# Moving the sample units of the third attention group into the mix stage, in a hybrid decoder step on eight cores

## The chip, the cores and the metric

The program runs on all eight cores of one Trainium2 chip; each core takes half a prompt sequence and four of the 32 sample sequences. The metric is the device time of the slowest core in microseconds (us). In the profiles PE is TensorE (matrix products; PEld its weight loads), DVE is VectorE, ACT ScalarE, POOL GpSimd and SP SyncE; here the last two mostly issue loads. TensorE writes its results to PSUM banks, from which DVE or ScalarE *evicts* them. Cores 0 to 3 are one die, 4 to 7 the other. Most executions agree within a fraction of a per cent, but the program also has a slow state, in which the cores of a die show a lower granted clock and the time is some per cent longer. Spans and stage lengths come from the profile of one execution, which covers every core.

## The reference, cut to what matters

One decoder layer. A wide input projection gives a GLU branch (depthwise convolution, layer norm, `w_pw`), queries, keys and values of three head groups with dilations 1, 4 and 16, and two gates. The branches are mixed, projected by `w_out`, and followed by a SwiGLU FFN.

```python
z = h @ w_in                               # [glu | q | k | v | gate_conv | gate_attn]
conv_out, new_conv = conv_branch(u, u_past, w_dw, b_dw, ln_g, ln_b, w_pw, b_pw)
o_att, new_k, new_v = attend(q, k, v)      # three groups, combined per head
attn_out = o_att @ w_o_att
x = x + (gate_conv * conv_out + gate_attn * attn_out) @ w_out
x = x + (silu(hf @ w_gate) * (hf @ w_up)) @ w_down
```

The four new tokens of each sample sequence attend to cached keys and values. The kernel cuts this into *units*: for each group 17 K units (load a 128x512 piece of the key cache and a broadcast query row, multiply, reduce), one exponential, and 17 V units (load a piece of the value cache, weight it, add it up by a small matmul). A K unit loads 512 KB, a V unit 256 KB. Group 1 shares some pieces; groups 2 and 3 load every one, so group 3 loads about 13 MB.

## The kernel before

The stages in order of time are: q and K/V passes of groups 1, 2 and 3; the GLU stage with the convolution; layer norm; the mix stage (48 iterations of gates, `w_pw` product, `w_o` product); `w_out`; FFN. Each engine has one instruction list and executes it in order (for DVE the timeline below shows it), so a wait in front of an instruction holds up everything behind it. All unit loads go through one issuing queue (SP), and units are put into *slots* between the other instructions:

```python
seq = [('K',) + u for u in cunits(0)]
for g in (0, 1):                             # V units of one group alternate with K units of the next
    seq.append(('E', g, 0, 0))
    for u0, u1 in zip(cunits(g), cunits(g + 1)):
        seq += [('V',) + u0, ('K',) + u1]
seq += [('E', 2, 0, 0)] + [('V',) + u for u in cunits(2)]
# ... K and Q have three buffers each, V two
def unit_slot(budget=1.4):                   # about one K unit with one V unit, or two V units
    u_pe()                                   # small matmuls of finished V units
    while used < budget and ...:
        u_prefetch()                         # loads, up to six units ahead, as far as buffers are free
        u_do(tptr['do'])                     # DVE work of this unit
    u_prefetch()
```

So K units of group 3 ran in its K/V pass and its V units in the GLU stage:

```python
# K/V passes of groups 2 and 3
def qslot():   ...  if qs[0] in (3, 5, 7): unit_slot()
def kslotA(i): if g == 1 or i > 0:  unit_slot()
def kslotB(i): if g == 1 or i >= 8: unit_slot()
# GLU stage: in each of 8 channel blocks x 3 column groups
unit_slot()
if tptr['do'] == len(seq) and n < 7:  ...    # then the sample normalisation
if n == 0 and ti > 0:
    prompt_norm(2 * ti - 2); prompt_norm(2 * ti - 1)   # load a denominator row, multiply
```

The mix stage used two alternating pairs of PSUM banks and loaded `w_pw` and `w_o` together per block of 256 columns. The `w_out` stage read chunks of 512 columns, two at a time; the first two were loaded during mix.

```python
b0, b1 = 4 + 2 * q, 5 + 2 * q                # mix(it), q = it % 2
if it == 35: wo.append(load_out(0))
if it == 41: wo.append(load_out(1))
# after mix: load_out(2), load_out(3), then 8 MB of residual rows
for p in range(2):
    for t in range(8):
        for c in (2 * p, 2 * p + 1):
            acc_rows(t, c, ...)
```

The softmax here doesn't subtract the row's maximum and nothing guards it: scores larger than these inputs give would overflow.

## Time and profile before

| | before |
|---|---|
| time, median of the first three runs | 2130.14 us (2126.32 to 2364.76; the longest is a slow run) |
| spans of the eight cores in the profile | 2097.5 to 2133.8 us |
| TensorE busy, slowest core | 2006.9 us, 94% |

Three lines of the page of the slowest core (core 3): busy time and share of TensorE, then the busy tenths of TensorE and the granted clock in 40 slices of 53 us (counted from 0 below).

```profile
PE 2006.9 (94%) x12908; PEld 1176.8 (55%) x12908; DVE 792.7 (37%) x1378; ACT 411.2 (19%) x764; POOL 132.8 (6%) x140
...
PE   5899989996779999999999999999999999999996
...
PEclk9999999998889999999999999999999999999998
```

TensorE is the bottleneck, and after the start it loses time mainly in slices 9 to 11, about 480 to 640 us: the third group's K/V pass and the GLU stage. The windows view of these two stages on core 3 (window, its length, busy time and instructions of TensorE, weight loads, DVE, ScalarE and GpSimd; then clock, DMA share, GB/s):

```profile
361.40:524.70 163.30, 146.88 (x835) 92.24 (x833) 76.87 (x181) 42.41 (x86) 4.56 (x4) 0.95 0.72 141
524.70:719.50 194.80, 161.06 (x1299) 93.55 (x1298) 69.37 (x112) 39.91 (x78) 9.13 (x8) 0.91 0.57 109
```

The chain of waits there (start, length, what) is mostly loads for units:

```profile
450.65 11.44 DMA t_67<-ck
...
476.00 12.71 DMA t_66<-ck
...
491.68 12.20 DMA t_73<-cv
...
506.10 15.74 DMA t_68<-sqkv
...
546.67 5.72 DMA t_130<-dnd
...
557.78 11.01 DMA t_131<-dnd
```

`ck` and `cv` are the caches, `sqkv` the new sample rows, `dnd` the softmax denominators of the prompt. The timelines of DVE and TensorE on core 3 show how such a wait arrives there, and that it is paid twice (in brackets the idle time before an instruction, and what ended it):

```profile
488.87 0.69 DVE L212 TENSOR_TENSOR t_74<-t_66,t_69 128x512 f32<-128x512 f32 x1 [4.25 <-DMA t_66<-ck]
...
490.75 0.26 DVE L212 TENSOR_TENSOR t_58<-ps,t_58 128x64 f32<-128x64 f32 x1
```

```profile
484.68 3.67 PE L212 MATMUL ps<-t_54,t_56 128*128 128x512 bf16 x16
491.15 0.63 PE L212 MATMUL ps<-t_90,t_95 128*128 128x64 bf16 x4 [2.81 <-DVE t_58 L212]
...
492.68 5.96 PE L212 MATMUL ps<-t_55,t_56 128*128 128x512 bf16 x16
```

DVE waits 4.25 us for a key load before it can do the work that TensorE needs (`t_58`). TensorE idles 2.81 us behind DVE, and the next sixteen matmuls of this size span 5.96 us instead of 3.67. The windows view shows why, a granted clock (third figure from the end) of 0.50:

```profile
490.60:497.40 6.80, 6.25 (x21) 2.78 (x22) 3.30 (x9) 1.38 (x3) 0.00 (x0) 0.50 0.92 114
```

The Trainium skill, page "TensorE: Matmul & The Clock Gate", section "Why this matters for your kernels", advises against idle gaps above about 3 us because the clock then drops; here 2.8 us (up to the modelled end of the matmul before) were followed by that lower clock.

### The profile page before, as it was taken

The page shows a single profiled execution, that of the slowest core. Times are in us where ns is not written, and L with a number is a line of the kernel's source. Part 1 is how long each engine was busy: PE and PEld are TensorE (multiplying, and loading weights), DVE is VectorE, ACT ScalarE, POOL GpSimd, SP SyncE. Part 2 cuts the span into 40 slices and gives each one's busy share as a digit, 9 for nine tenths or more (in the row PEclk, how much of TensorE's full clock was granted, in tenths as well). Part 3 has the DMA queues.
Part 4 walks back from the last instruction along what each step waited for, and adds up shares of the span by engine and source line. Part 5 has one row for each costly group of instructions (what it writes and reads, how often), then busy time and mean ns, then how long its engine had stood idle before and what let it go on. Part 6 is the DMA issues. An engine that isn't in the chain of part 4 may idle for free.

```text
span 2133.8 us, 34104 instructions; the slowest of 8 cores (2097.5 to 2133.8 us)
## 1 busy us (share of the span) xinstructions
PE 2006.9 (94%) x12908; PEld 1176.8 (55%) x12908; DVE 792.7 (37%) x1378; ACT 411.2 (19%) x764; POOL 132.8 (6%) x140
## 2 busy tenths in 40 slices
PE   5899989996779999999999999999999999999996
PEld 3454544663445556666545655656556556565652
DVE  4544564454324372222225143241441432414125
ACT  4353221321112252222104200000000000000012
POOL 0100000000000101101000000000000000000000
PEclk9999999998889999999999999999999999999998
DMA  8849788668548774747593999879879786454403
GB/s 217 159 123 152 113 159 139 117 156 157 133 78 137 110 99 56 107 56 102 107 229 45 184 157 184 133 138 172 139 139 164 127 152 97 71 78 63 79 23 138
DMA packets 228534, 266.31 MB, mean 125 GB/s; under 512 B 8867, under 2 KB 192803, under 8 KB 223229
## 3 DMA queue, kind: packets, MB, share of 16 engines
q0 software_dynamic: 190080, 130.03, 45.6%
q1 hardware_dynamic: 33686, 86.02, 15.6%
q10 hardware_dynamic: 4608, 48.08, 9.6%
q8 instruction: 106, 1.74, 0.3%
q14 instruction: 54, 0.44, 0.1%
HBM read 369.64 MB, written 60.30 MB: 201 GB/s over the span
## 4 chain that ended last, share of the span: by engine, by line
PE 83%; DMA 7%; DVE 4%; issue 3%; ACT 2%; SPq 1%; ACTq 1%; DVEq 0%; POOL 0%; POOLq 0%
PE ps L212 83%; DMA t_53<-w_in 1%; DMA t_73<-cv 1%; DMA t_68<-ck 1%; DMA t_68<-sqkv 1%; SPq L233 1%; DMA t_66<-ck 1%; DMA t_67<-ck 1%; DMA t_131<-dnd 1%; DMA t_59<-xext 1%; ACTq L233 0%; DMA t_125<-t_127 0%; DVE t_138 L212 0%; DVE t_63 L212 0%; DVE t_137 L212 0%
## 5 line engine op out<-in xcount | busy, mean ns | idle before, releaser
L212 PE MATMUL ps<-t_56,t_53 128*128 128x347 bf16 (+3 forms) x1152 | 180.4, 316 | 10.1 <-DVE t_127 L212 9.2
L212 PE MATMUL ps<-t_56,t_54 128*128 128x347 bf16 (+3 forms) x1152 | 183.3, 319 | 3.7 <-ACT t_157 L212 1.1
L212 PEld LDWEIGHTS ps<-t_56,t_53 128*128 128x128 bf16 x1152 | 112.9, 99 | 73.3 <-issue 13.9
L212 PEld LDWEIGHTS ps<-t_56,t_54 128*128 128x128 bf16 x1152 | 114.0, 100 | 68.7 <-issue 7.4
L212 PE MATMUL ps<-t_55,t_56 128*128 128x512 bf16 (+1 forms) x640 | 150.7, 390 | 0.0
L212 PE MATMUL ps<-t_54,t_56 128*128 128x512 bf16 (+1 forms) x640 | 145.4, 381 | 1.1 <-DVE t_56 L212 1.1
L212 ACT ACTIVATE t_192<-ps 128x347 f32<-128x347 f32 (+1 forms) x66 | 30.3, 460 | 535.9 <-PE ps L212 535.9
L212 PE MATMUL ps<-t_53,t_56 128*128 128x512 bf16 (+1 forms) x432 | 105.6, 400 | 4.6 <-DMA t_53<-w_in 4.6
L212 PEld LDWEIGHTS ps<-t_55,t_56 128*128 128x128 bf16 (+1 forms) x640 | 75.3, 122 | 57.7 <-issue 11.4
L212 PEld LDWEIGHTS ps<-t_54,t_56 128*128 128x128 bf16 (+1 forms) x640 | 74.9, 122 | 53.6 <-issue 4.0
L212 PE MATMUL ps<-t_136,wh_175 128*128 128x347 bf16 (+1 forms) x576 | 91.0, 311 | 0.5 <-DVE t_136 L212 0.5
L212 PE MATMUL ps<-t_136,wh_174 128*128 128x347 bf16 (+1 forms) x576 | 90.9, 311 | 0.0
L212 PE MATMUL ps<-t_136,wh_176 128*128 128x347 bf16 (+1 forms) x576 | 90.8, 311 | 0.0
L212 PE MATMUL ps<-t_136,wh_173 128*128 128x347 bf16 (+1 forms) x576 | 90.8, 311 | 0.0
L212 ACT ACTIVATE t_193<-ps 128x347 f32<-128x347 f32 (+1 forms) x66 | 30.3, 459 | 277.8 <-PE ps L212 277.8
L212 PE MATMUL ps<-t_136,wh_169 128*128 128x347 bf16 (+1 forms) x480 | 75.7, 311 | 0.0
L212 PE MATMUL ps<-t_136,wh_171 128*128 128x347 bf16 (+1 forms) x480 | 75.7, 311 | 0.0
L212 PE MATMUL ps<-t_136,wh_170 128*128 128x347 bf16 (+1 forms) x480 | 75.7, 311 | 0.0
L212 PE MATMUL ps<-t_136,wh_172 128*128 128x347 bf16 (+1 forms) x480 | 75.7, 311 | 0.0
L212 PEld LDWEIGHTS ps<-t_53,t_56 128*128 128x128 bf16 (+1 forms) x432 | 42.7, 102 | 57.7 <-issue 17.6
L212 DVE TENSOR_TENSOR t_190<-ps,t_192 128x347 bf16<-128x347 f32 (+1 forms) x36 | 18.7, 520 | 149.1 <-PE ps L212 149.1
L212 DVE TENSOR_TENSOR t_190<-ps,t_193 128x347 bf16<-128x347 f32 (+1 forms) x36 | 18.7, 520 | 147.7 <-PE ps L212 147.7
(408 smaller groups left out, 2910.8 us busy)
## 6 DMA issues: line engine op xcount, KB each, us to landing
t_54<-w_in POOLq DMA_DIRECT2D x14, 1024.0 KB, 15.4
t_53<-w_in POOLq DMA_DIRECT2D x12, 1024.0 KB, 13.9
kso<-ck ACTq DMA_DIRECT2D x8, 1016.0 KB, 11.4
vso<-cv ACTq DMA_DIRECT2D x8, 1016.0 KB, 10.0
t_59<-xext SPq DMA_DIRECT2D x6, 1024.0 KB, 10.0
t_53<-w_in POOLq DMA_DIRECT2D x12, 512.0 KB, 16.1
t_60<-xext SPq DMA_DIRECT2D x6, 1024.0 KB, 8.3
wh_175<-w_gate POOLq DMA_DIRECT2D x6, 1024.0 KB, 10.1
```

The source lines that it names most:

```text
L212: self.q[eng].append(lambda e: getattr(e, meth)(*a, **kw).then_inc(s, 1))
L233: self.q[queue].append(lambda e: e.dma_start(out=out, in_=in_, **kw).then_inc(s, 16))
```

## The change

The intent is to take the third group's units out of the stretch that stalls and put them into the mix stage, where DVE is mostly idle (busy 4.4 of 19.2 us in the windows view). Their buffers are columns of `hT` (now called `yA`) that nobody needs any more; V units of this group get three buffers instead of two. To make room, `w_o` is loaded whole and early, in the GLU stage; the mix stage uses one pair of PSUM banks; the sample rows' `w_o` product follows at the end of mix. As the whole `w_o` lies where the first `w_out` chunk used to go, only one chunk is loaded during mix, and the first pass of `w_out` takes chunk 0 for all rows and then chunk 1. Denominator rows are asked for earlier, and the unit slots move.

```diff
+seq = [('K',) + u for u in cunits(0)] + [('E', 0, 0, 0)]
+for u0, u1 in zip(cunits(0), cunits(1)):
+    seq += [('V',) + u0, ('K',) + u1]
+seq += [('E', 1, 0, 0)] + [('V',) + u for u in cunits(1)]
+n_early = len(seq)
+seq += [('K',) + u for u in cunits(2)] + [('E', 2, 0, 0)] + [('V',) + u for u in cunits(2)]
...
-    last = q_pass(g, pre, qslot)
+    last = q_pass(g, pre, nothing)
-    if g == 1 or i >= 8:                     # second slot of a block
+    if g == 1 or i >= 5:
...
-    unit_slot()                              # in the GLU stage
-    if n == 0 and ti > 0:
-        prompt_norm(2 * ti - 2); prompt_norm(2 * ti - 1)
+    if n == 1: prompt_norm(ti)               # loads issued in the first block, four buffers
+    if n == 2 and ti == 0: prompt_norm(3)
...
+    if ph == 2: S.dma('pool', wo4, w_o...)   # whole w_o
...
-    b0, b1 = 4 + 2 * q, 5 + 2 * q            # mix; now PS[4] and PS[5] only
+    if it > ND: unit_slot(1.4, len(seq))     # ND = 9
...
-    if it == 35: wo.append(load_out(0))
-    if it == 41: wo.append(load_out(1))
+    if it == 41: wo.append(load_out(0))
+wo.append(load_out(1))                       # after the last iteration
+mix_sample()                                 # 64 products with 16 columns
...
-    for t in range(8): for c in (2 * p, 2 * p + 1): ...
+    # p == 0: c = 0 for all t, then c = 1 for all t; p == 1 as before
```

More of the change, by code (lines that the diff above doesn't have):

```diff
@@ L527, in cunits, with ubuf @@
             return [(g, s, i) for s in range(4) for i in range(4)] + [(g, 4, 0)]
-        seq = [('K',) + u for u in cunits(0)]
-        for g in (0, 1):
-            seq.append(('E', g, 0, 0))
-            for u0, u1 in zip(cunits(g), cunits(g + 1)):
-                seq += [('V',) + u0, ('K',) + u1]
-        seq += [('E', 2, 0, 0)] + [('V',) + u for u in cunits(2)]
+        seq = [('K',) + u for u in cunits(0)] + [('E', 0, 0, 0)]
[4 more added lines that the diff above has]
+        seq += [('K',) + u for u in cunits(2)] + [('E', 2, 0, 0)] + [('V',) + u for u in cunits(2)]
         bufs, free, users = [], [], {}
-        ctr = {'K': -1, 'Q': -1, 'V': -1}
+        ctr = {}
         for t, (kind, g, s, i) in enumerate(seq):
             fresh = not (g == 0 and s < 4 and i > 0)
+            late = g == 2
             b_ = {}
-            fr = -1
-            for nm, n_, new in (('K', 3, fresh), ('Q', 3, True)) if kind == 'K' else (('V', 2, fresh),) if kind == 'V' else ():
+            fr = n_early - 1 if late else -1
+            for nm, n_, new in (('K', 3, fresh), ('Q', 3, True)) if kind == 'K' else (('V', 3 if late else 2, fresh),) if kind == 'V' else ():
+                c_ = ctr.get((nm, late), -1) + (1 if new else 0)
+                ctr[(nm, late)] = c_
                 if new:
-                    ctr[nm] += 1
-                    fr = max(fr, users.get((nm, ctr[nm] % n_), -1))
-                b_[nm] = ctr[nm] % n_
-                users[(nm, b_[nm])] = t
+                    fr = max(fr, users.get((nm, late, c_ % n_), -1))
+                b_[nm] = c_ % n_
+                users[(nm, late, c_ % n_)] = t
             bufs.append(b_)
             free.append(fr)
+        yA = v3(S.sbuf('yA', H_, 16 * HP), 16)
+        def ubuf(nm, g, i):
+            if g < 2:
+                return {'K': uK, 'Q': uQ, 'V': uV, 'P': [uP], 'PV': uPV}[nm][i]
+            if nm == 'PV':
+                return hT[:, 10 + i // 2, 512 * (i % 2):512 * (i % 2) + 512]
+            return yA[:, {'K': 0, 'Q': 3, 'V': 6, 'P': 9}[nm] + i, 0:512]
         def u_load(t):
@@ L553, in u_load @@
             if kind == 'K':
-                Q_, K_ = uQ[b_['Q']], uK[b_['K']]
+                Q_, K_ = ubuf('Q', g, b_['Q']), ubuf('K', g, b_['K'])
                 if s == 4:
@@ L562, in u_load @@
             elif kind == 'V':
-                V_ = uV[b_['V']]
+                V_ = ubuf('V', g, b_['V'])
                 if s == 4:
@@ L573, in u_do @@
             if kind == 'K':
-                P_ = uP[0:np_]
-                S.op('dve', lambda e: e.tensor_tensor(out=P_, in0=uK[b_['K']][0:np_], in1=uQ[b_['Q']][0:np_], op=ALU.mult))
+                P_ = ubuf('P', g, 0)[0:np_]
+                S.op('dve', lambda e: e.tensor_tensor(out=P_, in0=ubuf('K', g, b_['K'])[0:np_], in1=ubuf('Q', g, b_['Q'])[0:np_], op=ALU.mult))
                 dst = SnA[0:64, g, :] if s == 4 else ScA[:, g, 16 * s + 4 * i:16 * s + 4 * i + 4]
@@ L589, in u_do @@
                 pc = PnA[0:64, g, :] if s == 4 else PcA[:, g, 16 * s + 4 * i:16 * s + 4 * i + 4]
-                PV_ = uPV[pv_][0:np_]
-                S.op('dve', lambda e: e.tensor_tensor(out=v3(PV_, 4), in0=v3(uV[b_['V']][0:np_], 4), in1=mkap(pc, [[1, 4], [0, 128]]), op=ALU.mult))
+                PV_ = ubuf('PV', g, pv_)[0:np_]
+                S.op('dve', lambda e: e.tensor_tensor(out=v3(PV_, 4), in0=v3(ubuf('V', g, b_['V'])[0:np_], 4), in1=mkap(pc, [[1, 4], [0, 128]]), op=ALU.mult))
                 upend.append((uslot[0], PV_, g, s, i))
@@ L598, in build_program @@
         avail = [False] * 3
+        late_ok = [False]
         def u_pe(lag=2):
@@ L608, in u_prefetch, with unit_slot @@
         def u_prefetch():
-            while tptr['load'] < len(seq) and tptr['load'] <= tptr['do'] + 6 and avail[seq[tptr['load']][1]] and free[tptr['load']] < tptr['do']:
+            while tptr['load'] < len(seq) and tptr['load'] <= tptr['do'] + 6 and avail[seq[tptr['load']][1]] and free[tptr['load']] < tptr['do'] and (tptr['load'] < n_early or late_ok[0]):
                 u_load(tptr['load'])
                 tptr['load'] += 1
-        def unit_slot(budget=1.4):
+        def unit_slot(budget=1.4, lim=None):
             uslot[0] += 1
@@ L617, in unit_slot @@
             used = 0.0
-            while used < budget and tptr['do'] < len(seq) and avail[seq[tptr['do']][1]]:
+            while used < budget and tptr['do'] < (lim or n_early) and avail[seq[tptr['do']][1]]:
                 u_prefetch()
@@ L825, in pre @@
                     fin[0]()
-            qs = [0]
-            def qslot():
-                qs[0] += 1
-                if qs[0] in (3, 5, 7):
-                    unit_slot()
             def kslotA(i):
@@ L850, in build_program @@
         dgc = [ab(w2t + 1568 + 512 * i, 512).rearrange("p (q c) -> p q c", c=32) for i in range(2)]
-        PcS = v3(af(w2t + 2592, 512), 16)
         wtap = v3(af(w2t + 3104, 256), 8)
@@ L854, in build_program @@
         ysum, ysq = v3(af(R, 1056), 2), v3(af(R + 1056, 1056), 2)
-        stT = [v3(af(R + 10240, 480), 4), v3(af(w2t + 3376, 480), 4)]
-        cps = af(R + 11264, 1024)
-        osn = ab(R + 12288, 256)
+        stT = [v3(af(R + 5120 + 480 * i, 480), 4) for i in range(2)]
+        cps = af(R + 7334, 1024)
+        wo4 = v3(ab(R + 8448, 4096), 4)
         uc = [v3(af(R + 20552 + 136 * i, 136), 4) for i in range(2)]
@@ L862, in build_program @@
         sg = af(R + 20192, 360)
-        rdb = [af(R + 16688 + 1024 * i, 1024) for i in range(2)]
-        PnS, rds = af(R + 21752, 4), af(R + 21756, 4)
-        yA = v3(S.sbuf('yA', H_, 16 * HP), 16)
+        rdb = v3(af(R + 8448, 4096), 4)
+        PcS = v3(yA[:, 12, 0:512], 16)
+        osn = hT[:, 13, 0:512]
+        ta_s, cv_s = v3(yA[:, 14, 0:256], 16), v3(yA[:, 14, 256:512], 16)
+        PnS, rds = af(R + 21752 + 16, 4), af(R + 21756 + 16, 4)
         yv = [yA[:, 2 * n:2 * n + 2, 0:528] for n in range(8)]
@@ L875, in prompt_recip @@
                 S.dma('sp', dnd[h:h + 1, :], den[32 * h:32 * h + 1, :], writes=[('dn', h)])
+            for h in range(4):
+                S.dma('sp', rdb[:, h, :], dnd[h:h + 1, :].partition_broadcast(128), reads=[('dn', h)])
         def prompt_norm(h):
-            S.dma('sp', rdb[h % 2], dnd[h:h + 1, :].partition_broadcast(128), reads=[('dn', h)])
-            S.op('dve', lambda e: e.tensor_tensor(out=oT[:, h, 0:1024], in0=rdb[h % 2], in1=num[:, h, :], op=ALU.mult))
+            S.op('dve', lambda e: e.tensor_tensor(out=oT[:, h, 0:1024], in0=rdb[:, h, :], in1=num[:, h, :], op=ALU.mult))
         def sample_norm():
@@ L970, in build_program @@
                     prompt_recip()
+                    u_pe(0)
+                    assert tptr['do'] == n_early
                 S.op('act', lambda e: e.activation(out=sg[:, 0:nc_], in_=PS[pb][:, 0:nc_], func=AF.Sigmoid, bias=vcol(R_BGLU + 8 + n)))
@@ L984, in build_program @@
                         rows_out(n - 1)
-                unit_slot()
-                if tptr['do'] == len(seq) and n < 7:
-                    if upend:
-                        u_pe(1)
-                    else:
-                        next(sn, None)
                 if n == 0 and ti == 1:
                     state_T()
-                if n == 0 and ti > 0:
-                    prompt_norm(2 * ti - 2)
-                    prompt_norm(2 * ti - 1)
+                if n == 1:
+                    prompt_norm(ti)
+                if n == 2 and ti == 0:
+                    prompt_norm(3)
                 if ti == 2 and n > 0:
@@ L1008, in build_program @@
                     gates_load(ph - 2)
+                    if ph == 2:
+                        S.dma('pool', wo4, w_o.rearrange("(k p) n -> p k n", p=128))
         cT = v3(ab(R + 14624, 4160), 8)
         mixT = v3(ab(R, 8448), 16)
-        tt = [af(R + 8448 + 528 * i, 528) for i in range(2)]
+        tt = [af(R + 18784 + 528 * i, 528) for i in range(2)]
         o = R + 18784
-        tcb = [af(o + 352 * i, 352) for i in range(2)]
-        pwb = [af(o + 704 + 352 * i, 352) for i in range(2)]
-        t2b = [af(o + 1408 + 352 * i, 352) for i in range(2)]
-        tab_ = [af(o + 2112 + 352 * i, 352) for i in range(2)]
+        tcb = [af(o + 348 * i, 348) for i in range(2)]
+        tab_ = [af(o + 696 + 348 * i, 348) for i in range(2)]
+        pwb = [af(o + 1392 + 348 * i, 348) for i in range(2)]
+        t2b = af(o + 2088, 348)
         ND = 9
@@ L1023, in build_program, with w2_view @@
         its = [(n, c0, nc_) for n in range(16) for (c0, nc_) in TGN]
-        def w2_views(jh):
-            w2a = W[2][:, 3072 * (jh % 2):3072 * (jh % 2) + 2048].rearrange("p (k n) -> p k n", k=8)
-            w2b = W[2][:, 3072 * (jh % 2) + 2048:3072 * (jh % 2) + 3072].rearrange("p (k n) -> p k n", k=4)
-            return w2a, w2b
+        def w2_view(jh):
+            return W[2][:, 2048 * (jh % 2):2048 * (jh % 2) + 2048].rearrange("p (k n) -> p k n", k=8)
         def w2_load(jh):
-            w2a, w2b = w2_views(jh)
-            cs = slice(256 * jh, 256 * (jh + 1))
-            S.dma('pool', w2a, w_pw[:, cs].rearrange("(k p) n -> p k n", p=128))
-            S.dma('pool', w2b, w_o[:, cs].rearrange("(k p) n -> p k n", p=128))
+            S.dma('pool', w2_view(jh), w_pw[:, 256 * jh:256 * (jh + 1)].rearrange("(k p) n -> p k n", p=128))
         def tanhs(it):
@@ L1053, in mix @@
             wsl = slice((n % 2) * 128, (n % 2) * 128 + 128)
-            w2a, w2b = w2_views(n // 2)
-            b0, b1 = 4 + 2 * q, 5 + 2 * q
+            w2a = w2_view(n // 2)
             tc, ta = tanhs(it)
+            np_ = min(nc_, 1024 - c0)
             for k in range(8):
-                S.op('pe', lambda e: e.matmul(PS[b0][:, 0:nc_], lhsT=w2a[:, k, wsl], rhs=cT[:, k, c0:c0 + nc_], start=(k == 0), stop=(k == 7)))
+                S.op('pe', lambda e: e.matmul(PS[4][:, 0:nc_], lhsT=w2a[:, k, wsl], rhs=cT[:, k, c0:c0 + nc_], start=(k == 0), stop=(k == 7)))
@@ L1059, in mix @@
             for k in range(4):
-                S.op('pe', lambda e: e.matmul(PS[b1][:, 0:nc_], lhsT=w2b[:, k, wsl], rhs=oT[:, k, c0:c0 + nc_], start=(k == 0), stop=(k == 3)))
-            S.op('act', lambda e: e.activation(out=pwb[q][:, 0:nc_], in_=PS[b0][:, 0:nc_], func=AF.Identity, bias=vcol(R_BPW + n)))
-            S.op('dve', lambda e: e.scalar_tensor_tensor(out=t2b[q][:, 0:nc_], in0=ta[:, 0:nc_], scalar=1.0, in1=PS[b1][:, 0:nc_], op0=ALU.add, op1=ALU.mult))
+                S.op('pe', lambda e: e.matmul(PS[5][:, 0:np_], lhsT=wo4[:, k, 128 * n:128 * n + 128], rhs=oT[:, k, c0:c0 + np_], start=(k == 0), stop=(k == 3)))
@@ L1063, in mix @@
+            S.op('act', lambda e: e.activation(out=pwb[q][:, 0:nc_], in_=PS[4][:, 0:nc_], func=AF.Identity, bias=vcol(R_BPW + n)))
+            S.op('dve', lambda e: e.scalar_tensor_tensor(out=t2b[:, 0:np_], in0=ta[:, 0:np_], scalar=1.0, in1=PS[5][:, 0:np_], op0=ALU.add, op1=ALU.mult))
             S.op('dve', lambda e: e.scalar_tensor_tensor(out=pwb[q][:, 0:nc_], in0=tc[:, 0:nc_], scalar=1.0, in1=pwb[q][:, 0:nc_], op0=ALU.add, op1=ALU.mult))
-            S.op('dve', lambda e: e.tensor_tensor(out=mixT[:, n, c0:c0 + nc_], in0=pwb[q][:, 0:nc_], in1=t2b[q][:, 0:nc_], op=ALU.add))
@@ L1066, in stat_mm @@
-        def stat_mm(b, hf, a, nc_):
-            S.op('pe', lambda e: e.matmul(PS[b][:, 0:nc_], lhsT=onesf, rhs=ysum[:, hf, a:a + nc_], start=True, stop=True))
-            S.op('pe', lambda e: e.matmul(PS[b + 1][:, 0:nc_], lhsT=onesf, rhs=ysq[:, hf, a:a + nc_], start=True, stop=True))
-        def stat_ev(b, hf, a, nc_):
+            S.op('dve', lambda e: e.tensor_tensor(out=mixT[:, n, c0:c0 + np_], in0=pwb[q][:, 0:np_], in1=t2b[:, 0:np_], op=ALU.add))
+            if np_ < nc_:
+                S.op('act', lambda e: e.copy(out=ta_s[:, n, :], in_=ta[:, np_:nc_]))
+                S.op('act', lambda e: e.copy(out=cv_s[:, n, :], in_=pwb[q][:, np_:nc_]))
@@ new lines, in mix_sample @@
+        def mix_sample():
+            for n in range(16):
+                for k in range(4):
+                    S.op('pe', lambda e: e.matmul(PS[6][:, 16 * n:16 * n + 16], lhsT=wo4[:, k, 128 * n:128 * n + 128], rhs=oT[:, k, 1024:1040], start=(k == 0), stop=(k == 3)))
+            S.op('dve', lambda e: e.scalar_tensor_tensor(out=ta_s, in0=ta_s, scalar=1.0, in1=v3(PS[6][:, 0:256], 16), op0=ALU.add, op1=ALU.mult))
+            S.op('dve', lambda e: e.tensor_tensor(out=mixT[:, :, 1024:1040], in0=ta_s, in1=cv_s, op=ALU.add))
@@ L1072, in stat_ev, with stat_mm @@
+        def stat_mm(hf, a, nc_, *pl):
+            for (b_, o_), src in zip(pl, (ysum, ysq)):
+                S.op('pe', lambda e: e.matmul(PS[b_][:, o_:o_ + nc_], lhsT=onesf, rhs=src[:, hf, a:a + nc_], start=True, stop=True))
+        def stat_ev(hf, a, nc_, *pl):
             m_, v_, t_ = ysum[:, hf, a:a + nc_], ysq[:, hf, a:a + nc_], tt[0][:, 0:nc_]
-            S.op('dve', lambda e: e.tensor_scalar(out=m_, in0=PS[b][:, 0:nc_], scalar1=1.0 / 1024, scalar2=None, op0=ALU.mult))
+            s1, s2 = [PS[b_][:, o_:o_ + nc_] for b_, o_ in pl]
+            S.op('dve', lambda e: e.tensor_scalar(out=m_, in0=s1, scalar1=1.0 / 1024, scalar2=None, op0=ALU.mult))
@@ L1074, in stat_ev @@
             S.op('dve', lambda e: e.tensor_tensor(out=t_, in0=m_, in1=m_, op=ALU.mult))
-            S.op('dve', lambda e: e.scalar_tensor_tensor(out=v_, in0=PS[b + 1][:, 0:nc_], scalar=1.0 / 1024, in1=t_, op0=ALU.mult, op1=ALU.subtract))
+            S.op('dve', lambda e: e.scalar_tensor_tensor(out=v_, in0=s2, scalar=1.0 / 1024, in1=t_, op0=ALU.mult, op1=ALU.subtract))
         def ln_rstd(hf):
@@ L1088, in ln_apply @@
                 S.op('act', lambda e: e.activation(out=cT[:, n, 512 * hf:512 * hf + w_], in_=t_, func=AF.Silu, scale=vcol(R_LNG + n), bias=vcol(R_LNB + n)))
-        assert not upend and next(sn, None) is None
+        assert not upend
         gates_load(1)
@@ L1104, in build_program @@
         gate(3)
-        stat_mm(6, 0, 0, 512)
-        stat_mm(4, 1, 0, 264)
-        stat_ev(6, 0, 0, 512)
+        st1, st2, st3 = (0, 0, 512, (4, 0), (5, 0)), (1, 0, 256, (6, 0), (6, 256)), (1, 256, 272, (4, 0), (5, 0))
+        stat_mm(*st1)
+        stat_mm(*st2)
+        stat_ev(*st1)
         gate(4)
-        stat_mm(6, 1, 264, 264)
-        stat_ev(4, 1, 0, 264)
-        stat_ev(6, 1, 264, 264)
+        stat_mm(*st3)
+        stat_ev(*st2)
+        stat_ev(*st3)
         ln_rstd(0)
@@ L1127, in load_out @@
         def load_out(c):
-            dst = FW[(c + 3) % 4].rearrange("p (k n) -> p k n", k=16)
+            dst = FW[(0, 1, 3, 2)[c]].rearrange("p (k n) -> p k n", k=16)
             S.dma('pool', dst, w_out[:, 512 * c:512 * (c + 1)].rearrange("(k p) n -> p k n", p=128))
@@ L1132, in build_program @@
         wo = []
+        late_ok[0] = True
         for it in range(48):
@@ L1135, in build_program @@
                 gate(it)
+                if it > ND:
+                    if tptr['do'] < len(seq) or upend:
+                        unit_slot(1.4, len(seq))
+                    else:
+                        next(sn, None)
             mix(it)
@@ L1141, in build_program @@
                 w2_load(jh + 2)
-            if it == 35:
+            if it == 41:
                 wo.append(load_out(0))
-            if it == 41:
-                wo.append(load_out(1))
+        assert next(sn, None) is None and not upend and tptr['do'] == len(seq)
+        wo.append(load_out(1))
+        mix_sample()
         HW = [S.sbuf('wh%d' % i, W_OFF[i // 2] + 2048 * (i % 2), 2048, BF16) for i in range(8)]
@@ L1234, in build_program @@
         for p in range(2):
-            for t in range(8):
-                for c in (2 * p, 2 * p + 1):
+            for t, cs in ([(t, (c,)) for c in (0, 1) for t in range(8)] if p == 0 else [(t, (2, 3)) for t in range(8)]):
+                for c in cs:
                     acc_rows(t, c, (lm, lambda k, c_: wo[c_][:, k, :]), KC, pctr[0] % 6)
@@ L1254, in ring @@
         def ring(src2d, kc):
-            dst = HW[(hctr[0] + 6) % 8].rearrange("p (k n) -> p k n", k=kc)
+            dst = HW[hctr[0] % 8].rearrange("p (k n) -> p k n", k=kc)
             hctr[0] += 1
```

## The prediction

> **What bounds the kernel.** TensorE is 94% busy over a span of 2134 us (busy table); its losses lie before 720 us. The mix stage (800 to 1110 us) and the FFN are at 98 to 100%. The windows view gives 410 to 620 us: PE busy 167 of 210 us, granted clock 0.89. The chain of waits there is a string of loads for the sample units (cv, ck, sqkv, dnd: 5 to 20 us each) with short DVE multiplies between. DVE executes in order, so a unit waiting for its load holds up the rope and GLU evictions that TensorE needs. Stalls are paid twice: sixteen 128x512 matmuls span 3.6 us normally, 5.0 to 6.0 after a stall. The Trainium skill, "TensorE: Matmul & The Clock Gate", "Why this matters for your kernels", says pauses above about 3 us lower the clock; this trace agrees (0.74 to 0.83 in the idlest 20 us windows).
>
> **Gained.**
> - GLU stage, 524.7 to 719.5 us: 195 us. Once the units are gone (from 640 us) a channel block takes 19.3 us. Eight blocks, the first shorter: about 153. Gain about 40, including earlier denominator loads (5 to 11 us waits in the chain).
> - End of the second group and queries of the third: unit waits of 6.6, 4.6 and 3.2 us at 310 to 330 us, plus slow clock, cost about 16 us; three slots fewer should leave one wait. Gain 12.
> - Third group's K/V pass: 163 us against about 133 without stalls (16 blocks of 8.2). Group 3's K units go, but group 2's V units now all run there, two per slot, with two buffers. A V load takes 6 to 8 us, a slot about 4: eight or nine slots at about 7 us leave some 22 us of stall. Gain 0 to 8, 4 taken.
>
> **Added or moved.**
> - Mix stage: unit and normalisation products, about 6 us of TensorE, move there. DVE (4.4 of 19.2 us busy) has room; loads run three units ahead. DMA share rises from about 0.57 to 0.87: 3 us of stalls.
> - PS4/PS5 single-buffered: about 0.3 us in each of the first nine iterations, which have no gate: 2.5 us.
> - Sample product of w_o: 64 small products at about 57 ns (as the 128x128 transposes), minus 0.4: 3 us.
> - w_out: chunk 1 is asked for only at the end of mix, where the first chunk asked for took 42 us to land (beside 8 MB of residual rows). It is needed about 33 us later: 9 us of stall plus 2 of slow clock. Before, a two-chunk pass of 55 us covered it.
>
> **Sum.** 40+12+4-6-3-2.5-3-11 = 30.5; I take 33 us, nearly all on the TensorE path: 2097 us, 0.985 of before, range 2070 to 2122. Chances: faster by over 2% 0.34, within 2% 0.64, slower 0.02.
>
> **What would show it.** GLU stage near 153 us with almost no DVE waits for cv or dnd; third group's K/V pass still 150 to 165 us, DVE waiting for group 2's cv; mix about 12 us longer, its first nine iterations at 2.1 us instead of 1.77; TensorE waiting 8 to 10 us for a w_out chunk after the first eight row blocks.
>
> **What would make it wrong.** V loads below 5 us: the K/V pass gains up to 20 us and the whole is over 2%. The chunk landing in under 33 us: 11 us better. Gate weights delayed by 80 GB/s of unit loads: they have 39 us to land and take 14 to 25; if late, each of about four column blocks stalls several us. Conv shift copies delayed by the early 4 MB w_o load: a few us.

## The result, and the profile after

| | before | after |
|---|---|---|
| time, median (four runs each, one chip) | 2132.55 us (one of the four is a slow run) | 2102.9 us (2100.67 to 2105.72) |
| ratio of fast runs | | 0.9871, interval 0.9842 to 0.9901 |
| spans of the cores in the profile | 2097.5 to 2133.8 | 2083.1 to 2099.1 |

Ratios here and below are the mean time of one kernel's fast runs over that of the other's of the same rounds, so not quite the ratio of the medians quoted. The predicted ratio was 0.985. The means of the fast runs, 2130.5 and 2103.1 us, differ by 27 us where 33 were forecast; the medians differ by 30, but the one of before counts its slow run. The kernel is faster by 1.3%, so within the 2% to which the prediction gave a chance of 0.64.

The page of core 3 (2099.0 us; the slowest, core 6, took 2099.1), same lines:

```profile
PE 1998.0 (95%) x12972; PEld 1175.9 (56%) x12972; DVE 793.2 (38%) x1380; ACT 417.5 (20%) x797; POOL 127.5 (6%) x133
...
PE   6899997999999899999799999999999999999996
...
PEclk9999999999999999999899999999999999999998
```

The gap at slices 9 to 11 is closed, and a new one stands in slice 19, about 1000 to 1050 us. The dip in slice 6, about 315 to 370 us, is the end of group 2, where waits remain (below). The windows of the two stages on core 3, as for before:

```profile
364.20:505.30 141.10, 139.27 (x840) 91.68 (x837) 65.87 (x163) 41.44 (x82) 4.56 (x4) 1.00 0.56 118
505.30:659.40 154.10, 147.88 (x1248) 88.64 (x1246) 56.64 (x86) 40.81 (x79) 9.89 (x9) 0.99 0.67 124
```

The clock is back at 1.00 and 0.99, and DMA share in the K/V pass fell from 0.72 to 0.56. Of the string of loads in the chain one is left (core 6):

```profile
359.92 103.14 PE ps L212 x614
...
463.88 4.30 DMA t_72<-cv
...
471.95 17.85 PE ps L212 x111
```

For the whole comparison one core is not enough, because before's cores differ by 16 us in the GLU stage alone. The table gives stage lengths, from the first matmul of a stage to that of the next, as medians over the cores. (In the first two rows six cores are used; in the records of the other two 51 early matmuls are missing, which shifts those bounds.) Medians need not add up to the change of the time.

| stage | predicted change | before | after | change |
|---|---|---|---|---|
| K/V pass of group 2 with q pass of group 3 | -12 | 151.7 | 147.2 | -4.5 |
| K/V pass of group 3 | -4 | 159.8 | 141.3 | -18.5 |
| GLU | -40 | 182.1 | 156.4 | -25.7 |
| layer norm | 0 | 55.3 | 53.1 | -2.2 |
| mix, first nine iterations | +2.5 | 20.7 | 25.6 | +4.9 |
| mix, the rest, with the sample product | +12 | 253.1 | 259.7 | +6.6 |
| `w_out` | +11 | 121.5 | 135.5 | +14.0 |
| FFN to the end | 0 | 963.5 | 963.2 | -0.3 |

The new gap is the second `w_out` chunk. First TensorE's timeline on core 6, then the DMA list (size, time from issue to landing), and the DMA list of before for the same place:

```profile
997.43 27.79 PE L212 MATMUL ps<-wf_162,t_134 128*128 128x512 bf16 x128
1039.64 30.09 PE L212 MATMUL ps<-wf_163,t_134 128*128 128x512 bf16 x128 [14.42 <-DMA wf_163<-w_out]
```

```profile
wf_163<-w_out POOLq DMA_DIRECT2D x1, 2048.0 KB, 44.6
wf_165<-w_out POOLq DMA_DIRECT2D x1, 2048.0 KB, 57.7
wf_164<-w_out POOLq DMA_DIRECT2D x1, 2048.0 KB, 68.0
```

```profile
wf_166<-w_out POOLq DMA_DIRECT2D x1, 2048.0 KB, 42.1
wf_167<-w_out POOLq DMA_DIRECT2D x1, 2048.0 KB, 59.0
```

Before, the chunk that landed 42.1 us after its issue had 58 us of other work in front of it; now the one that lands after 44.6 us has about 30.

### The profile page after: what moved, and what is told of

It reads as the page before. It is cut to its first block, busy times and chain, and to the rows that moved or that the text cites. A ratio compares the mean times of both kernels' runs of the same rounds, so it can differ in the third digit from the quotient of the medians.

```text
span 2099.0 us, 34195 instructions; the slowest of 8 cores (2083.1 to 2099.1 us)
## 1 busy us (share of the span) xinstructions
PE 1998.0 (95%) x12972; PEld 1175.9 (56%) x12972; DVE 793.2 (38%) x1380; ACT 417.5 (20%) x797; POOL 127.5 (6%) x133
## 4 chain that ended last, share of the span: by engine, by line
PE 87%; DMA 5%; DVE 3%; issue 2%; ACT 2%; SPq 0%; DVEq 0%; ACTq 0%; POOL 0%; POOLq 0%
PE ps L212 87%; DMA wf_163<-w_out 2%; DMA t_68<-ck 1%; DMA t_53<-w_in 1%; DMA t_61<-xext 0%; DVE t_136 L212 0%; DMA t_125<-t_127 0%; DVE t_63 L212 0%; DVE t_135 L212 0%; DVE t_56 L212 0%; ACT t_63 L212 0%; SPq L233 0%; DVE xacc_181 L212 0%; ACT t_191 L212 0%; ACT t_64 L212 0%
## 5 line engine op out<-in xcount | busy, mean ns | idle before, releaser
L212 PE MATMUL ps<-t_56,t_54 128*128 128x347 bf16 (+3 forms) x1152 | 178.9, 314 | 7.1 <-DVE t_126 L212 3.3
L212 PE MATMUL ps<-t_56,t_53 128*128 128x347 bf16 (+3 forms) x1152 | 177.3, 312 | 1.3 <-DVE t_126 L212 0.7
```

Of the source, the lines that this page charges most:

```text
L212: self.q[eng].append(lambda e: getattr(e, meth)(*a, **kw).then_inc(s, 1))
```

## The experiments

Twelve experiments ran. The three that leave out or redirect loads give wrong sample rows; the others gave correct results. In the experiments' traces the tile names have lost their numbers (`t` for `t_74`). Theory A was that DVE waits for unit loads and, being in order, holds up TensorE. Rival B was the units' own work, rival C the bytes themselves.

### Before, without the third group's loads

```diff
 def u_load(t):
+    if g == 2: return
```

> The kernel before, with the loads of the third group's units left out (the units multiply what lies in their buffers; the sample rows come out wrong on purpose). All DVE and TensorE work stays where it was. Theory A (DVE waits for these loads, and holds up the evictions behind it): third group's K/V pass falls from 160 us (median over the cores) to 135-142, the GLU stage from 182 to 160-165 (unit products and denominator waits stay), in all 2085-2095 us. Rival B (the units' own DVE and TensorE work is what costs): both stages stay within 5 us, above 2120 us.

Measured: ratio to before 0.9806 (0.9782 to 0.983), that is about 41 us less. K/V pass 148.1 us, GLU 164.2. The profiled execution was disturbed on core 0 alone (clock 0.497, span 4095 us), and there only in the FFN; the other seven cores ran at a clock of 0.982 or more, and the medians over the cores do not rest on core 0.

Rival B falls as the main cause: all the work is still there, and most of the time is gone. The K/V pass missed its range (135 to 142) by 6 us. Against the changed kernel (141.3 and 156.4) 7 and 8 us are left in the two stages; the units' own work, which stays here, and the waits that remain (on core 3, in the K/V pass, 4.5 us for `cv` and 1.4 for sample rows) were not separated.

### Before, with these loads sent to a scratch area of HBM

```diff
+scr = nc.dram_tensor('scr', [51 * 128, 512], F32).ap()
-Q_, K_ = uQ[b_['Q']], uK[b_['K']]
+Q_, K_ = (sc_[0], sc_[1]) if g == 2 else (uQ[b_['Q']], uK[b_['K']])     # V likewise
```

> The kernel before, with the same loads of the third group's units issued at the same places, but into a scratch area of HBM, so that no unit waits for them (wrong sample rows on purpose). Theory A (waiting in order on DVE): as fast as without the loads, within 10 us, K/V pass 135-145, GLU 160-168. Rival C (13 MB of loads take bandwidth from the conv copies and the GLU weights): stays near before, K/V pass above 152, GLU above 175.

Measured: ratio 0.9968 (0.9936 to 1.0; only two of the four runs were fast). K/V pass 164.3 us (156.0 to 177.0 over the cores), GLU 171.1, between the ranges of theory A and rival C. No unit of group 3 waits for anything, and still the K/V pass is, by the median, as slow as before. DVE's waits for loads in that stage on core 3, before and here (waiting tile, what for; total us, times, longest):

```profile
DVE t_74 L212 <- DMA t_67<-ck: 9.7, 4, 3.8
DVE t_74 L212 <- DMA t_66<-ck: 9.2, 3, 4.2
DVE t_74 L212 <- DMA t_68<-sqkv: 4.4, 1, 4.4
DVE t_74 L212 <- DMA t_68<-ck: 3.6, 2, 2.7
DVE t_78 L212 <- DMA t_73<-cv: 0.7, 1, 0.7
```

```profile
DVE t L212 <- DMA t<-cv: 15.0, 7, 3.8
DVE t L212 <- DMA t<-sqkv: 6.1, 1, 6.1
```

On this core the pass is 5.6 us shorter than before (163.3 to 157.7). On core 5 it is 8.0 us longer (157.7 to 165.7), and the same line reads:

```profile
DVE t L212 <- DMA t<-cv: 23.7, 6, 9.2
```

The waits for group 3's keys are gone and waits for group 2's *values* have taken their place. Theory A was thus half the story: DVE's order carries the delay to TensorE, but what makes the loads late is the amount asked for in this stretch (rival C). Remove the waiters and leave the bytes, and other waiters pay. In the GLU stage 11 of the 18 us saved without loads are saved here too, so waiting on group 3's own loads counts for more there. One reservation: the destination is HBM instead of the core's memory. In the window from 350 to 720 us on core 3 the issuing queue moved the same 29.98 MB in both kernels and held the DMA engines for 34.4% of the time, against 35.4% before. But V loads into the core's memory, which both kernels have in this K/V pass, landed later here: 7.6 to 12.1 us after their issue (medians of six cores, of the loads whose landing the trace shows), against 4.9 to 8.0 before and 2.8 to 3.4 in the kernel without the loads (only five such landings a core). Late loads thus follow the traffic, but the redirected traffic weighed more than the original, so the 164.3 us may overstate the share of the bytes.

### The changed kernel with the old unit slots

```diff
-last = q_pass(g, pre, nothing)
+last = q_pass(g, pre, qslot)                # three slots in the q passes of groups 2 and 3
-if g == 1 or i >= 5:
+if g == 1 or i >= 8:
```

> The changed kernel with the old unit slots (three in each q pass of groups 2 and 3, second slot of a block of group 3 only from block 8). The prediction held that giving up the q-pass slots saves 12 us at the end of group 2 and in the q pass of group 3; the traces show 4.6 us (K/V of group 2 111.5 to 108.5, q pass 39.9 to 38.3). Expected: those two stages 2-6 us longer, the K/V pass of group 3 about the same or 3 us shorter, as fewer units are left for it; whole kernel within 6 us of the changed one.

Measured: ratio 0.9902 (0.9864 to 0.9941). Group 2's pass and the q pass 149.3 us, against 147.2 and 148.6 in two profiles of the changed kernel; K/V pass of group 3 139.7. The slots' own worth is 1 to 2 us, at the limit of what the profiles resolve.

### The changed kernel with late denominator loads

```diff
 def prompt_norm(h):
+    S.dma('sp', rdb[:, h, :], dnd[h:h + 1, :].partition_broadcast(128), reads=[('dn', h)])
```

It is called at the old places in the first block, still with four buffers.

> The changed kernel with the denominator rows loaded at the point of use again (DVE waits for them in the first GLU block, as before). If the denominator waits were a part of the gain in the GLU stage, that stage grows from 156 to 162-168 us. If they mattered only beside the unit loads, it stays within 3 us of 156.

Measured: GLU 156.0 us; ratio 0.9873 (0.9841 to 0.9905). DVE waits 0.8 to 1.4 us for `dnd` on the four cores looked at (1, 3, 5 and 7). It waited 15 to 17 us on the same cores before, and 4.3 to 4.5 us in the kernel without the third group's loads. The denominator waits in before's chain were mostly a consequence of the load traffic; asking earlier gained nothing by itself.

### The changed kernel with two pairs of banks in the first nine mix iterations

```diff
+b0, b1 = (0, 1) if it < ND and q else (4, 5)
```

> The changed kernel with two pairs of PSUM banks in the first nine mix iterations (odd ones use banks 0 and 1, free of gates by then). Theory: the single pair costs those iterations 5 us (20.7 before, 25.6 after), by 4.7 us before the second iteration and 0.2-0.4 us in each later one. Expected: 20-22 us for the nine iterations, whole kernel 4-5 us below the changed one. Rival: the moved buffers or the early w_o weights cost it; then 25 us stay.

Measured: the nine iterations 22.0 us (median of the cores) instead of 25.6, so most of the loss is the single pair. TensorE's timeline, before (core 3) and after (core 6):

```profile
774.95 1.34 PE L212 MATMUL ps<-t_135,t_55 128*128 128x347 bf16 x8
776.13 0.75 PE L212 MATMUL ps<-t_107,t_55 128*128 128x347 bf16 x4
776.72 0.90 PE L212 MATMUL ps<-t_135,t_55 128*128 128x347 bf16 x5
778.30 0.31 PE L212 MATMUL ps<-t_135,t_55 128*128 128x347 bf16 x1 [0.68 <-ACT t_135 L212]
```

```profile
712.04 1.34 PE L212 MATMUL ps<-t_133,t_55 128*128 128x347 bf16 x8
713.22 0.75 PE L212 MATMUL ps<-t_107,t_121 128*128 128x347 bf16 x4
718.70 2.48 PE L212 MATMUL ps<-t_133,t_55 128*128 128x347 bf16 x8 [4.73 <-ACT t_141 L212]
...
727.11 1.35 PE L212 MATMUL ps<-t_133,t_55 128*128 128x347 bf16 x8 [0.20 <-ACT t_142 L212]
```

ScalarE in the latter (`t_133` is the layer norm's output there, `t_141` the first iteration's eviction):

```profile
717.29 0.83 ACT L212 ACTIVATE t_133<-t_136,t_51 128x528 bf16<-128x528 f32 x1 [0.61 <-DVE t_136 L212]
718.03 0.53 ACT L212 ACTIVATE t_141<-ps,t_51 128x347 f32<-128x347 f32 x1
```

With two pairs the second iteration starts at once and takes each row of `t_135` (the layer norm's output in before) as it comes. With one pair it must wait until ScalarE has evicted the first iteration, and ScalarE does that only after all its layer norm work: 4.73 us of idleness, slow matmuls after it, then 0.2 to 0.4 us each time.

The whole kernel did not gain: ratio 0.9889 (0.9843 to 0.9934). Its mix stage took 263 to 275 us on four cores, with TensorE waiting for `w_pw` weights.

### The changed kernel with most of the second chunk loaded early

Since `w_o` left the third weight buffer, half of it lies unused during mix.

```diff
-dst = FW[(0, 1, 3, 2)[c]]...
+dst = FW[(0, 2, 1, 3)[c]]...                 # chunk 1 into the third weight buffer
+if it == 35: load_out(1, 8, 16)              # rows k 8 to 15
 if it == 41:
     wo.append(load_out(0))
+    load_out(1, 0, 4)
-wo.append(load_out(1))
+wo.append(load_out(1, 4, 8))                 # 1 MB left for the end
```

The cut leaves out that the FFN's weight buffers are taken in another order. The 1 MB counts what is read (four bytes an element); as written it is half of that, as are the 2048 KB of a chunk in the DMA list above.

> The changed kernel with the second w_out chunk placed where three quarters of it can be loaded before the mix stage ends (k 8-15 from iteration 35, k 0-3 from 41), only 1 MB is left for its end. Theory: TensorE waits 14.4 us because this chunk is asked for at the end of mix, beside 8 MB of residual rows, and lands 44.6 us later. Expected: no wait at the second chunk, first half of w_out 57-59 us instead of 71, whole kernel 12-15 us below the changed one. If mix gets longer by the earlier loads, by under 2 us.

Measured: first half of `w_out` 57.2 us, whole stage 121.9, as before the change; time 2099.45 us median (2092.41 to 2105.19), ratio 0.9839 (0.9798 to 0.988). The wait is gone, and 13.6 us of the stage with it. The time falls by less than that, and its interval overlaps those of the changed kernel (0.9871 and 0.9903): in the profile one core again waits for `w_pw` in mix (269.1 us).

### The changed kernel with half of the residual rows held back

```diff
-S.dma('sp', xacc[t], xext[...])
+S.dma('sp', xacc[t], xext[...], after=[otok[1]] if t >= 4 else [])   # after chunk 1 has landed
```

> The changed kernel, with residual rows 4 to 7 loaded only after the second w_out chunk has landed. If the chunk is late because the residual rows share the bandwidth, it lands in 25-33 us instead of 44.6, and the wait of 14.4 us falls to 0-4 us, some of it given back as evictions waiting for residual rows; whole kernel 8-14 us below the changed one. Rival: the chunk's own queue is slow (descriptors of 2 KB rows): it lands at about 40 us or later all the same and nothing is gained.

Measured: the chunk lands 25.9 to 31.3 us after its issue on the eight cores (39.5 to 44.6 in the changed kernel), so it was late because it shared the bandwidth. But the whole stage is 134.1 us, 1.4 us less than with the plain change, and the ratio is 0.9915 (0.9897 to 0.9932). The wait has moved to later rows and to a later chunk; core 0's timeline:

```profile
1047.94 15.94 PE L212 MATMUL ps<-wf,t 128*128 128x512 bf16 x128 [1.24 <-DVE xacc L212]
1070.14 13.17 PE L212 MATMUL ps<-wf,t 128*128 128x512 bf16 x48 [6.26 <-DMA wf<-w_out]
```

After mix there is too much to load at once: of what was tried here, bringing bytes forward helped, changing their order did not.

### The changed kernel without the last three slots of group 2's K/V pass

```diff
-if g == 1 or i > 0:                          # first slot of a block
+if (g == 1 and i < 11) or (g == 2 and i > 0):
-if g == 1 or i >= 5:                         # second slot
+if (g == 1 and i < 10) or (g == 2 and i >= 5):
```

> The changed kernel without the last three unit slots of group 2's K/V pass (those units move to group 3's pass, which has six slots to spare). Theory: the three waits of 3.1, 4.9 and 5.0 us at 314 to 330 us are for loads that share the bandwidth with 8 MB of weights for group 3, and giving up q-pass slots did not touch them. Expected: end of group 2 and q pass of group 3 together 8-12 us shorter (146.8 to 135-139), K/V pass of group 3 2-5 us longer; whole kernel 4-8 us below the changed one. Rival: the queries of group 3 are late because their weights are; then nothing moves.

Measured: group 2's pass and the q pass 133.0 us, 14 less, so the three unit waits were the loss there. The K/V pass of group 3 grew from 141.3 to 151.6, more than twice what was expected. It got three more K units (nine loads of cached keys instead of six on core 3), which is the likely cause; its DVE now waits 10.6 us for sample rows (core 3). The ratio, 0.9872 (0.9844 to 0.99), is that of the changed kernel: given back one stage later. Here are the three waits in the changed kernel (DVE timeline, core 6), which the prediction had counted as mostly gone:

```profile
314.45 0.69 DVE L212 TENSOR_TENSOR t_74<-t_66,t_69 128x512 f32<-128x512 f32 x1 [3.12 <-DMA t_66<-ck]
...
322.09 0.69 DVE L212 TENSOR_TENSOR t_74<-t_67,t_70 128x512 f32<-128x512 f32 x1 [4.89 <-DMA t_67<-ck]
...
330.44 0.69 DVE L212 TENSOR_TENSOR t_74<-t_68,t_71 128x512 f32<-128x512 f32 x1 [5.03 <-DMA t_68<-ck]
```

### The changed kernel again

> The changed kernel itself once more, as the neighbour of the next three on one chip. Its first profile had 259.7 us for the mix stage after its first nine iterations on every core; the profiles of four variants that leave this stage alone show 265 to 275 us on one to four of their cores, with TensorE waiting 6 to 12 us for w_pw weights. If that is a property of the change and not of the variants, some cores of this profile show it too, and the times lie between 2100 and 2117 us.

Measured: 2109.91 us median (2102.43 to 2115.12), ratio 0.9903 (0.9874 to 0.9933). Two of eight cores show the longer mix stage, 271.0 and 265.6 us. TensorE on core 3, in the window of that stage:

```profile
PE ps L212 <- DMA t<-w_pw: 8.2, 1, 8.2
```

So the wait is a property of the change. It strikes some cores in some executions, and the first profile happened to have none.

### The changed kernel without the unit loads in mix

```diff
 def u_load(t):
+    if g == 2: return
```

> The changed kernel with the loads of the third group's units left out of the mix stage (wrong sample rows on purpose; all DVE and TensorE work stays). Theory: the occasional wait for w_pw in mix comes from these loads, about 80 GB/s, sharing the bandwidth with the gate and w_pw weights. Expected: no wait for w_pw or w_in in mix on any core, 259.7 to 260 us on all eight, so the remaining 6.6 us over the 253.1 us of before are moved TensorE work. Rival: the new order of weight loads alone is too late; then waits stay on some cores.

Measured: 259.7 to 259.9 us on all eight cores, no DMA wait of TensorE on the core looked at; 2105.01 us median (2102.91 to 2106.81), ratio 0.9882 (0.9854 to 0.9909). The evidence fits the theory, but one profile without the wait is not proof of its cause, since the first profile of the changed kernel had none either.

### The changed kernel with w_pw in four slots

```diff
-return W[2][:, 2048 * (jh % 2):2048 * (jh % 2) + 2048]...
+return W[2][:, 2048 * (jh % 4):2048 * (jh % 4) + 2048]...
-if it % 6 == 5 and jh + 2 < 8: w2_load(jh + 2)
+if it % 6 == 5 and jh + 4 < 8: w2_load(jh + 4)    # and four blocks before mix
```

> The changed kernel with w_pw in four slots instead of two (w_o left the room), each loaded four column blocks ahead instead of two. If late w_pw loads are the only new wait in mix: 259.7 to 260.5 us on all cores, and a mean time 2-8 us below the changed kernel of this call, with less spread. If gate weights are late as well, waits for w_in take the place of those for w_pw and little is gained.

Measured: mix 259.7 to 259.9 us on all cores as expected, but 2107.73 us median (2103.67 to 2114.79), ratio 0.9898 (0.9872 to 0.9924), 1 us below the changed kernel of the same call. The expectation of 2 to 8 us is missed: the slowest core of this profile (2109.8 us) has an undisturbed mix stage. Whether the waits for `w_pw` cost the time of the slowest core anything is not shown.

### Three repairs together

The two pairs of banks, the four `w_pw` slots and the early chunk (its quarters loaded after iterations 29, 35, 41 and at the end).

> The changed kernel with three repairs together: two pairs of PSUM banks in the first nine mix iterations (measured 4 us), w_pw in four slots (2-8 us), and three quarters of the second w_out chunk loaded before the end of mix (14-15 us of the w_out stage). Expected 2078-2090 us, ratio to before 0.972 to 0.981. If the saved time comes back as waits in the first FFN block, that stage would grow from 64.3 us.

Measured: 2088.89 us median (2081.64 to 2104.99), ratio to before 0.9826 (0.9784 to 0.9868), against 0.9903 for the changed kernel: 21 us by the medians. The first nine iterations take 20.7 us, mix 259.7 to 259.9 on seven cores and 262.2 on one, `w_out` 123.0, FFN unchanged. It is the fastest correct kernel here, though two of its six runs lie above 2100 us, the median is at the edge of the expected range and the ratio just outside; what made those two slower is open. It is not distinguishable from the early chunk alone (0.9839, on another chip).

## Why the prediction was right or wrong

The time, 2102.9 us, lies near the forecast 2097 and inside its range. That it came so near is partly luck: the terms erred in both directions, by up to 14 us, and mostly cancelled (changes of -30.5 us forecast in sum, -25.7 measured as the sum of the medians).

**Cause: right, but incomplete.** The prediction put the losses on units that wait for their loads on an in-order DVE. The kernel without loads confirms it (41 us). The scratch kernel adds what it lacked: in the third group's K/V pass the lateness comes from the bytes asked for, and was seen to disappear only when they left the stretch.

**GLU, predicted -40, measured -25.7.** The end value was right (153 forecast, 156.4 measured). The start value was mis-sized: 195 us is the stage on the slowest core, whereas the eight cores took 179 to 195 with a median of 182.1. On core 3, from which it was read, the stage did go from 194.9 to 154.0.

**K/V pass of group 3, predicted -4, measured -18.5.** The step that failed: "eight or nine slots at about 7 us leave some 22 us of stall", which rests on "A V load takes 6 to 8 us". That time was read from loads that competed with the very traffic the change removes (4.9 to 8.0 us before, 2.8 to 3.4 without group 3's loads, see the scratch kernel). TensorE is busy 139.27 of 141.10 us in the window above, so the stall is about 2 us instead of 22. The length without stalls erred the other way, about 139 us instead of 133, so only part of the slip shows. In the changed kernel a V load issued at 444.83 us was used at 447.96, 3.1 us later (core 6, SP queue and DVE timeline):

```profile
444.83 0.33 SPq L233 DMA_DIRECT2D t_73<-cv  x1
...
447.96 0.69 DVE L212 TENSOR_TENSOR t_78<-t_73,t_80 128x512 bf16<-128x512 f32 x1 [1.51 <-DMA t_73<-cv]
```

The prediction named this as its first way to be wrong ("V loads below 5 us"). The Trainium skill, "DMA: Bandwidth & Descriptors", "Anatomy of one DMA — SWDGE (gpsimd) path", fits a DMA as 2.0 us plus bytes over 436 GB/s, which gives an estimate of 2.6 us for 256 KB; the fit is for the other kind of queue, but would have been nearer.

**End of group 2, predicted -12, measured -4.5.** The step that failed: "three slots fewer should leave one wait". Three waits of 3.1, 4.9 and 5.0 us remain, 13.0 in all (core 6), where before had 6.6, 4.6 and 3.2 (core 3). Why giving up three slots did not remove two of them is not shown; probably other units took their place in a stretch that also loads the next group's weights. Taking the last slots away did remove the waits (14 us), only to cost 10 us in the next pass.

**Mix, predicted +6 of moved work, +3 of sample product and +3 of stalls, measured +6.6.** The 64 small products took 1.6 us on core 6, from 995.8 to 997.4 us, 25 ns each, not 57. The 57 ns came from products with 128 columns; these have 16. The Trainium skill, "TensorE: Matmul & The Clock Gate", "Wait — 56ns, not 53.3ns?", gives a floor of about 25 ns between starts however small the matmul, which this trace matches. About 5 us are then moved unit work. The stalls exist, but only in some executions, and for `w_pw`, not for the gate weights named.

**First nine iterations, predicted +2.5, measured +4.9.** Only the small waits per iteration were counted; the first one, behind ScalarE's layer norm work, was missed.

**w_out, predicted +11, measured +14.0.** Mechanism and place were right: the chunk landed after 39.5 to 44.6 us, median 42.1, where 42 were assumed. The difference is in the time in front of it, 30 us (core 6) instead of the 33 forecast; 2 us of that are the shorter sample product (1.6 us instead of 64 times 57 ns).

## What to carry to other kernels

When loads are late, ask first how many bytes the stretch asks for: the instruction that waits is only the one whose turn it is, and removing it can pass the wait on. A latency measured under contention does not hold once the change removes the contention. Read a stage's length on all cores before forecasting what can be saved, and after moving work check where its buffers came from: here the room taken from `w_out` cost 14 us, and loading three quarters of one chunk earlier won them back.

## What the Trainium skill lacked or had wrong

- "DMA: Bandwidth & Descriptors", "Issuing engines are not separate DMA queues", says that DMAs of all engines interleave on the same 16 DMA engines. It has no figure for what that does to one transfer: the first 2 MB (as written) `w_out` chunk asked for at the end of mix landed after 39.5 to 44.6 us over the eight cores beside eight residual rows of 1 MB, and after 25.9 to 31.3 us with four of them held back. The trace agrees with the statement.
- No page that was looked up says that a wait passes from one stream of loads to another when the first stops being waited for but is still loaded. On core 3, sending group 3's loads elsewhere took away 22.5 us of DVE waits for cached keys and brought 15.0 us of waits for group 2's cached values, where there had been 0.7; on core 5 it took away 16.1 and brought 23.7, where there had been 0.6.
- "TensorE: Matmul & The Clock Gate", "Why this matters for your kernels", puts the harmful gap above about 3 us. Here a gap of 2.81 us was followed by a granted clock of 0.50 and sixteen matmuls in 5.96 us instead of 3.67; as the ends of matmuls are modelled, this is no clear contradiction. The page calls its windows free-running ("What's actually happening"); whether they are was not tested, but the stretches at 0.50 between 300 and 640 us on core 3 last 3.41, 6.83 or 10.24 us, whole multiples of 3.41.
- "TensorE: Matmul & The Clock Gate", "Wait — 56ns, not 53.3ns?": the floor of about 25 ns was right for 16-column products with a fresh 128x128 weight load each (1.6 us for 64).
